# Value weights folded into the output weights in the opening of the attention: first loads right behind the keys', four staging tiles, stores on ScalarE's queue

## The chip, the cores and the metric

The kernel runs on one core of one Trainium2 chip. A core has five engines, each with its own queue of instructions: TensorE (PE, with its weight loads shown apart as PEld), VectorE (DVE), ScalarE (ACT), GpSimd (POOL) and SyncE (SP), which here only issues transfers. The metric is device time in microseconds (us) of one execution, as the median of several. A transfer issued from the queue of ScalarE or SyncE occupies that queue for the issue alone and lands later.

## The reference, cut to what matters

The reference is one encoder layer on 2048 tokens of width 1024. What the change touches is the latent attention (group B) and the output projection:

```python
q  = (rms_norm(c_q, g_cq) @ w_uq).reshape(B, S, 4, 192)
kv = (rms_norm(c_kv, g_ckv) @ w_ukv).reshape(B, S, 4, 256)   # c_kv: 128 wide
k_nope, v = kv[..., :128], kv[..., 128:]                      # per head: key part, value part
...
p = softmax(q @ k.T * scale)                                  # 4 heads, 2048 x 2048
y_b = p @ v                                                   # per head 2048 x 128
x = x + concat(y_a, y_b) @ w_out                              # w_out: 1024 x 1024
x = x + relu(rms_norm(x) @ w_ff1)**2 @ w_ff2
```

Here y_a is the output of the mLSTM (group A), four heads scanned in both directions over chunks of 128 tokens. The last 512 rows of w_out, 128 for each head, multiply y_b.

## The kernel before, in words

**Products.** All large products are in fp32r. A value is cut into a high part (a cast on ACT) and a low part (a subtraction on DVE or POOL, the helper `split`), and `mm3` (L68 to L71) makes one product of three matmuls: high by high, high by low, low by high.

**Phase A** takes 16 tiles of 128 tokens in two halves of eight: RMSNorm of x, h @ W_in in blocks of columns (the matmuls into tiles `pz`), a convolution for the mLSTM's queries and keys, and for each tile the work of the latent attention in four ticks. `mla_a1` (L309) normalises the two latents into `cn` (columns 256 to 383 are the latent of keys and values) and transposes them; `mla_a2` (L332) makes keys and values (two PSUM banks of 512 columns, weights `wukh`/`wukl` of 1024 columns) and queries (two banks of 384); `mla_b1` (L364) copies the values from PSUM to `vn` on ACT and stores them to `d_va`; `mla_b2` (L391) normalises, rotates and stores queries and keys. In phase A a scheduler orders the instructions by their dependences.

**The attention** (L975 on) is written in an order by hand. The steps g run from 0 to 255, two at a time. Sixteen steps make one block of 512 queries of one head, and four such blocks one head. A pair of steps issues, in this order: two score tiles (five matmuls each, L1090 to L1094, into one of three PSUM banks; DVE evicts each at L1095), two products of probabilities and values (`pv`, from g = 22 on), softmax exponentials on ACT (L1106), eight transposes of probabilities into two banks (L1137, then a cast `pth` on ACT and a subtraction `ptl` on DVE), and two steps of a second stream of work, the mLSTM, which starts with a prelude of 28 steps (`mlstm_prelude`, L603 to L722) that computes the gates. The prelude takes its PSUM tiles `pm` in turn from two banks (pool `c_psM`), so each new tile waits until the one before the last has been read. At the end of the prelude are the steps called p2, p1, p4 and p3 below: p2 is copied to `x2`, p1 to `x1`, p4 (L712, made from `x2`) to `rv`, and p3 (L717) is made from `x1`.

**Values and keys of a head.** `load_v` and `split_v` bring the values of one head in four tiles, 16 in all; each costs a cast on ACT and a subtraction on POOL. When a head ends, the keys of the next are split: those of step u = 4 and 5 of the pair on POOL, those of u = 6 on DVE. After the attention come the output projection (`OutProj`, with w_out's rows) and the feed-forward in Strassen form.

## Time and profile before

| what | value |
| --- | --- |
| median of three runs | 2545.64 us (2544.19, 2545.64, 2546.84) |
| the profiled execution, its own time | 2542.08 us |
| its span | 2540.3 us |
| granted TensorE clock | 1.00 throughout |
| busy: TensorE, weight loads | 99%, 83% |
| busy: VectorE, ScalarE, GpSimd | 68%, 51%, 15% |
| moved by DMA | 392.53 MB, 155 GB/s in the mean |

The span is what the profile covers; the execution's own time has 1.8 us more around it. A busy share counts the time in which at least one instruction of the engine was running. Matmuls are pipelined, so two matmuls of one stream overlap in the records: the spacing of their starts tells what one of them costs, and the duration in a group's row does not. Phase A covers the first 460 us, the attention with the mLSTM about 460 to 1110 us, output projection and feed-forward the rest.

### The profile page before, as it was taken

The numbers are of one execution on the slowest core, as the hardware profiler recorded it, in microseconds if no ns is written. First come the engines' busy times: TensorE is split into PE (matmuls) and PEld (weight loads), VectorE is DVE, ScalarE is ACT, GpSimd is POOL, SyncE is SP. The second block draws the span as 40 slices with busy tenths as digits, with TensorE's granted clock in tenths as the row PEclk, the third lists the DMA queues.
The fourth block names the chain that finished last, engine by engine and source line by source line (L and its number), as shares of the span: only waits on it lengthen the run. The fifth ranks groups of instructions, "written<-read, shape, count | busy, mean of one in ns | idle before, by whom it ended". The sixth has DMA issues, their size and how long they took to land. (4 is left out here: it accounts for less than half of the span.)

```text
span 2540.3 us, 35812 instructions
## 1 busy us (share of the span) xinstructions
PE 2523.7 (99%) x12380; PEld 2111.3 (83%) x12380; DVE 1726.1 (68%) x3286; ACT 1293.7 (51%) x2900; POOL 380.7 (15%) x428
## 2 busy tenths in 40 slices
PE   9999999999999999999999999999999999999999
PEld 7888888788888888888888888888888888888887
DVE  5585467766667667678788777977775577665433
ACT  6454444656767677674455555655554323332332
POOL 1211111223323332200000000000000232322000
PEclk9999999999999999999999999999999999999999
DMA  5434234355344343235786555654448544444552
GB/s 177 143 112 152 91 113 137 111 146 134 89 115 114 85 121 102 63 110 193 235 271 227 196 189 185 244 166 149 142 153 300 201 149 142 145 145 145 211 183 95
DMA packets 295931, 392.53 MB, mean 155 GB/s; under 512 B 32262, under 2 KB 176965, under 8 KB 295749
## 3 DMA queue, kind: packets, MB, share of 16 engines
q1 hardware_dynamic: 293284, 385.78, 48.0%
q10 hardware_dynamic: 2464, 4.46, 0.5%
q8 instruction: 97, 1.59, 0.3%
q14 instruction: 86, 0.70, 0.1%
HBM read 258.51 MB, written 131.64 MB: 154 GB/s over the span
## 5 line engine op out<-in xcount | busy, mean ns | idle before, releaser
L69 PE MATMUL pd<-w2h,uh 128*128 128x512 f32 x896 | 348.8, 389 | 0.1
L70 PE MATMUL pd<-w2l,uh 128*128 128x512 f32 x896 | 348.7, 389 | 0.0
L71 PE MATMUL pd<-w2h,ul 128*128 128x512 f32 x896 | 348.7, 389 | 0.0
L54 DVE TENSOR_TENSOR ul<-ur,uh 128x1024 fp32r<-128x1024 f32 x110 | 149.3, 1357 | 251.8 <-ACT uh L53 251.8
L53 ACT CAST uh<-ur 128x1024 fp32r<-128x1024 f32 x110 | 115.7, 1052 | 396.0 <-PE pd L70 382.4
L54 DVE TENSOR_TENSOR ptl<-ptp,pth 128x512 fp32r<-128x512 f32 x248 | 171.1, 691 | 190.0 <-ACT pth L53 188.9
L53 ACT CAST pth<-ptp 128x512 fp32r<-128x512 f32 x248 | 143.4, 578 | 157.7 <-PE ptp L1137 157.1
L2015 DVE TENSOR_TENSOR e<-pu,e 128x512 f32<-128x512 f32 x224 | 151.3, 689 | 88.7 <-PE pu L71 87.7
L69 PEld LDWEIGHTS pd<-w2h,uh 128*128 128x128 f32 x896 | 168.2, 188 | 35.4 <-DVE e L2015 0.5
L71 PEld LDWEIGHTS pd<-w2h,ul 128*128 128x128 f32 x896 | 168.2, 188 | 34.9
L70 PEld LDWEIGHTS pd<-w2l,uh 128*128 128x128 f32 x896 | 168.2, 188 | 34.8
L1106 ACT ACTIVATE p<-p,nm 128x512 f32<-128x512 f32 x256 | 185.8, 726 | 2.6 <-DVE nm L1099 2.6
L1095 DVE TENSOR_SCALAR_CACHE_REDUCE p<-ps 128x512 f32<-128x512 f32 x256 | 167.4, 682 | 15.2 <-PE ps L1094 15.1
L2179 POOL TENSOR_TENSOR r<-wr,r 128x512 f32<-128x512 f32 x48 | 81.5, 1697 | 621.1 <-DMA wr<-in_w 590.0
L69 PE MATMUL pz<-wh,hh 128*128 128x512 f32 (+1 forms) x384 | 149.5, 391 | 1.7 <-ACT vo L495 0.7
L71 PE MATMUL pz<-wh,hl 128*128 128x512 f32 (+1 forms) x384 | 150.0, 391 | 0.0
L70 PE MATMUL pz<-wl,hh 128*128 128x512 f32 (+1 forms) x384 | 149.2, 389 | 0.1
L2018 ACT ACTIVATE e<-e 128x512 f32<-128x512 f32 x128 | 80.9, 632 | 120.5 <-DVE e L2015 114.0
L1137 PE MATMUL ptp<-ident,p 128*128 128x128 f32 x992 | 130.6, 274 | 0.5 <-DVE ptl L54 0.3
L1137 PEld LDWEIGHTS ptp<-ident,p 128*128 128x128 f32 x992 | 113.6, 140 | 14.1 <-issue 1.4
L1090 PE MATMUL ps<-kh,qh 128*128 128x512 f32 x256 | 112.8, 441 | 2.4 <-DVE p L1095 2.4
L1883 ACT CAST r<-w1raw 128x512 fp32r<-128x512 f32 x104 | 64.6, 622 | 92.5 <-PE pu L71 92.5
(526 smaller groups left out, 6463.5 us busy)
## 6 DMA issues: line engine op xcount, KB each, us to landing
d_u<-e SPq DMA_DIRECT2D x224, 256.0 KB
ur<-d_u SPq DMA_DIRECT2D x110, 512.0 KB
wr<-in_w SPq DMA_DIRECT2D x96, 256.0 KB
w1raw<-in_w SPq DMA_DIRECT2D x42, 512.0 KB
raw<-in_w_in SPq DMA_DIRECT2D x48, 256.0 KB
r<-in_w SPq DMA_DIRECT2D x22, 512.0 KB
mb<-d_M SPq DMA_DIRECT2D x32, 256.0 KB
acc<-d_x SPq DMA_DIRECT2D x16, 512.0 KB
```

The lines of the kernel that those rows point to most:

```text
L53: r = nc.scalar.copy(hi, src)
L54: (eng or nc.vector).tensor_tensor(lo, src, hi.bitcast(F32), op=ALU.subtract)
L69: nc.tensor.matmul(out, ah, bh, start=first, stop=False, skip_group_check=more)
L70: nc.tensor.matmul(out, ah, bl, start=False, stop=False, skip_group_check=more)
L71: nc.tensor.matmul(out, al, bh, start=False, stop=last, skip_group_check=more)
L1090: nc.tensor.matmul(o, qh[:, qs], kh, start=True, stop=False)
L1095: nc.vector.tensor_scalar(p, o, SCALE, None, op0=ALU.mult, op1=ALU.max, accum_out=maxes[b, a][:, j:j + 1])
L1106: nc.scalar.activation(p, p, AF.Exp, bias=maxes[b, a], accum_out=dens[b][:, a, j:j + 1])
L1137: nc.tensor.transpose(pt[:, k, :], p[:, k * P:(k + 1) * P], c.ident)
L2015: nc.vector.tensor_tensor(out, o, t, op=ALU.add)
L2018: nc.scalar.activation(t, t, AF.Relu)
L2179: nc.gpsimd.tensor_tensor(R, wr, R, op=ALU.subtract)
```

## The change

The values of all heads are products of one latent with columns of w_ukv, so p @ v @ w_out can be taken as (p @ latent) @ (value columns of w_ukv @ w_out's rows). The change computes that second bracket once, 512 x 1024, in the opening of the attention, and stores it as `d_wv`.

- In phase A `mla_a2` makes the 512 key columns only, with one `mm3` in place of two. `vn` and `d_va` are gone; the latent goes from `cn` to `d_cn` by one transfer for each tile, issued on ACT's queue. `cn` has one buffer. The pool of x tiles has three buffers in place of two, and the tiles 8 to 15 are loaded earlier.
- In the attention the values are the latent itself, four tiles for all heads, loaded at g = 2 to 8 and split at g = 16 to 22. At a change of heads the keys of u = 4 are split on POOL and those of u = 5 and 6 on DVE.
- `value_loads` brings the value columns of w_ukv and two pieces of w_out behind the keys' loads. `value_rows` scales the columns by the gain on POOL, transposes and splits them, and then makes eight pieces, each with a split of a piece of w_out (ACT and POOL), one `mm3` into a `pm` bank, a copy by DVE into one of four staging tiles `wst`, and a store on ACT's queue. Its steps run with the prelude's; pieces 0 to 3 have their products at steps 8, 10, 12 and 14, pieces 4 to 7 at 22, 24, 26 and 28.
- Output projection and `load_b2` read `d_wv` where they read the last 512 rows of w_out. The reloads of the mLSTM's keys and values are issued one step earlier.

```diff
     c.d_kr = dr.tile([NH, ROPE, S], F32, name="d_kr")
-    c.d_va = dr.tile([S, 512], F32, name="d_va")
+    c.d_cn = dr.tile([S, P], F32, name="d_cn")
+    c.d_wv = dr.tile([NH * P, D], F32, name="d_wv")
     c.d_ya = dr.tile([S, 512], F32, name="d_ya")
...
         kp = pool("a_mla_const", 1, "right")
-        xp = pool("a_x", 2, "right")
+        xp = pool("a_x", 3, "right")
         zp = pool("a_zr", 8, "right")
...
                 raw = rp.tile([P, 512], F32, name="raw")
-                cs = slice(j * 512, (j + 1) * 512)
-                nc.sync.dma_start(raw, c.w_ukv[:, cs])
-                split(nc, wukh[:, cs], wukl[:, cs], raw, gcq[:, 2:3])
+                nc.sync.dma_start(raw, c.w_ukv[:, j * 512:(j + 1) * 512])
+                cs = slice(j * 256, (j + 1) * 256)
+                split(nc, *[w[:, cs].rearrange("p (h d) -> p h d", h=2) for w in (wukh, wukl)],
+                      raw.rearrange("p (h t d) -> p h t d", h=2, t=2)[:, :, 0, :], gcq[:, 2:3])
...
                 split(nc, ch, cl, pt[:, 0:3, :])
-            mla_env[t] = [zr, ms3, ch, cl]
+            mla_env[t] = [zr, ms3, ch, cl, cn]
...
-            zr, ms3, ch, cl = mla_env[t]
-            pk, pq = [], []
-            for j in range(2):
-                o = psM.tile([P, 512], F32, name="pm")
-                cs = slice(j * 512, (j + 1) * 512)
-                mm3(nc, o, ch[:, 2, :], cl[:, 2, :], wukh[:, cs], wukl[:, cs], True, True)
-                pk.append(o)
+            zr, ms3, ch, cl, cn = mla_env[t]
+            nc.scalar.dma_start(c.d_cn[t * P:(t + 1) * P, :], cn[:, 256:384])
+            pq = []
+            pk = psM.tile([P, 512], F32, name="pm")
+            mm3(nc, pk, ch[:, 2, :], cl[:, 2, :], wukh[:, 0:512], wukl[:, 0:512], True, True)
             for j in range(2):
...
             qs = [pq[h // 2][:, (h % 2) * DH:(h % 2 + 1) * DH] for h in range(NH)]
-            ks = [pk[h // 2][:, (h % 2) * 256:(h % 2) * 256 + NOPE] for h in range(NH)]
+            ks = [pk[:, h * NOPE:(h + 1) * NOPE] for h in range(NH)]
             for h in range(NH):
...
             rsqrt(c, r8, ms8, 8)
-            mla_env[t] = [zr, pk, qs, ks, r8]
+            mla_env[t] = [zr, qs, ks, r8]
...
-            tok = slice(t * P, (t + 1) * P)
-            zr, pk, qs, ks, r8 = mla_env[t]
-            vn = mp.tile([P, NH, DV], F32, name="vn")
-            for j in range(2):
-                nc.scalar.copy(vn[:, 2 * j:2 * j + 2, :],
-                               pk[j].rearrange("p (h d) -> p h d", h=2)[:, :, NOPE:])
-            nc.sync.dma_start(c.d_va[tok, :], vn.rearrange("p h d -> p (h d)"))
+            zr, qs, ks, r8 = mla_env[t]
             kpe = mp.tile([P, 1, ROPE], F32, name="kpe")
...
                 norm(t, xt)
+            elif 8 <= t < 13:
+                xts[t + 3] = load_x(t + 3)
...
                     tick(n + 6 * half)
+                    if half == 0 and blk == 2 and i == 3:
+                        for t in range(8, 11):
+                            xts[t] = load_x(t)
                     if half == 0 and blk == 2 and i >= 4:
...
         yield
+def value_place(n):
+    h, j = divmod(n, 2)
+    return slice(h * P, (h + 1) * P), slice(j * 512, (j + 1) * 512)
+def value_loads(c, stage):
+    raw = stage.tile([P, 512], F32, name="raw").rearrange("p (h d) -> p h d", h=NH)
+    c.nc.sync.dma_start(raw, c.w_ukv.rearrange("p (h t d) -> p h t d", h=NH, t=2)[:, :, 1, :])
+    pieces = [stage.tile([P, 512], F32, name="raw") for _ in range(2)]
+    for n, t in enumerate(pieces):
+        c.nc.sync.dma_start(t, c.w_out[512:][value_place(n)])
+    return raw, dict(enumerate(pieces))
+def value_rows(c, pool, psM, raw, pieces):
+    nc = c.nc
+    tile = pool.tile
+    outs = [tile([P, 512], F32, name=f"wst{i}") for i in range(4)]
+    wvh, wvl = (tile([P, NH, P], F32R, name=f"wv{u}") for u in "hl")
+    homes = [[tile([P, 512], F32R, name=f"wo{i}{u}") for u in "hl"] for i in range(2)]
+    raws = [tile([P, 512], F32, name=f"wraw{i}") for i in range(2)]
+    def part(n):
+        if n < 2 * NH:
+            split(nc, *homes[n % 2], pieces.pop(n), eng=nc.gpsimd)
+        if n + 2 < 2 * NH:
+            pieces[n + 2] = raws[n % 2]
+            nc.sync.dma_start(raws[n % 2], c.w_out[512:][value_place(n + 2)])
+    nc.gpsimd.tensor_scalar(raw, raw, c.vec[:, 10:11], None, op0=ALU.mult)
+    for _ in range(5):
+        yield
+    pt = psM.tile([P, 512], F32, name="pm").rearrange("p (k t) -> p k t", k=4)
+    for h in range(NH):
+        nc.tensor.transpose(pt[:, h, :], raw[:, h, :], c.ident)
+    yield
+    split(nc, wvh, wvl, pt)
+    part(0)
+    yield
+    yield
+    done = None
+    for n in range(2 * NH):
+        o = psM.tile([P, 512], F32, name="pm")
+        mm3(nc, o, wvh[:, n // 2, :], wvl[:, n // 2, :], *homes[n % 2], True, True)
+        yield
+        w = outs[n % 4]
+        nc.vector.tensor_copy(w, o)
+        part(n + 1)
+        yield
+        nc.scalar.dma_start(c.d_wv[value_place(n)], w)
+        for _ in range(6 if n == 3 else 0):
+            yield
...
         outs = [outer(kws.pop(ch), ld.pop(ch)[0]) for ch in grp]
+        for ch in grp:
+            if ch > 4:
+                ld[ch - 4] = mlstm_v(c, ch - 4), mlstm_k(c, ch - 4)
         yield
...
                 nc.sync.dma_start(c.d_C[ch - 1], new)
-                ld[ch - 4] = mlstm_v(c, ch - 4), mlstm_k(c, ch - 4)
             if k == 0 and n + 1 < len(groups):
...
-        def load_v(h, j):
-            raw = vraw[h, j] = rp.tile([P, 512], F32, name="raw").rearrange("p (k d) -> p k d", k=4)
-            nc.sync.dma_start(raw, c.d_va[j * 512:(j + 1) * 512, h * DV:(h + 1) * DV].rearrange(
-                "(k p) d -> p k d", p=P))
-
-        def split_v(h, j):
-            raw = vraw.pop((h, j))
+        def load_v(j):
+            raw = vraw[j] = rp.tile([P, 512], F32, name="raw").rearrange("p (k d) -> p k d", k=4)
+            nc.sync.dma_start(raw, c.d_cn[j * 512:(j + 1) * 512, :].rearrange("(k p) d -> p k d", p=P))
+        def split_v(j):
+            raw = vraw.pop(j)
             vh = vp.tile([P, 4, DV], F32R, name="vh")
...
             split(nc, vh, vl, raw, eng=nc.gpsimd)
-            V[h, j] = vh, vl
+            V[j] = vh, vl
...
         def pv(b, j, k):
-            h = b // NB
             if (j, k) == (0, 0):
...
             th, tl = pts[b, j]
-            vh, vl = V[h, j]
+            vh, vl = V[j]
             if b < N - 1:
...
                 nc.gpsimd.memset(t[:, :, DV:], 1.0)
-            ld = {ch: (mlstm_v(c, ch), mlstm_k(c, ch)) for ch in range(NT - 1, NT - 5, -1)}
-            yield from mlstm_prelude(c, psM)
+            with ExitStack() as s_fold:
+                fold = value_rows(c, pool("w_sb", 1, "left", s_fold.enter_context), psM, *early)
+                for n, _ in enumerate(mlstm_prelude(c, psM)):
+                    next(fold, None)
+                    if n == 10:
+                        ld = {ch: (mlstm_v(c, ch), mlstm_k(c, ch)) for ch in range(NT - 1, NT - 5, -1)}
+                    yield
+                for _ in fold:
+                    yield
             yield from mlstm_steps(c, pool("l_sb", 1, "left", sl.enter_context), psM, ld)
...
             split_k(0, j, nc.gpsimd if j == 2 else nc.vector)
-        load_v(0, 0)
-        load_v(0, 1)
+        early = value_loads(c, rp)
         work = mlstm()
-        def next_v(bp, j):
-            h = bp // NB + 1
-            if bp % NB == NB - 1 and h < NH:
-                split_v(h, j)
-                if j < 2:
-                    load_v(h, j + 2)
-
         for g0 in range(0, 16 * N, 2):
...
                     pv(bp, *divmod(n, 4))
-                    if n % 4 == 3:
-                        next_v(bp, n // 4)
             if g0 % 16 == 4 and g0 > 32:
...
                 if h < NH - 1 and i == 7 and u in (4, 5, 6):
-                    split_k(h + 1, u - 3, nc.vector if u == 6 else nc.gpsimd)
-                    if u == 6:
-                        load_v(h + 1, 0)
-                        load_v(h + 1, 1)
+                    split_k(h + 1, u - 3, nc.gpsimd if u == 4 else nc.vector)
                 if g >= 16:
...
                         load_k(h + 1, u - 3)
-                if g in (6, 8, 10, 12):
-                    split_v(0, g // 2 - 3)
-                    if g < 10:
-                        load_v(0, g // 2 - 1)
+                if g in (2, 4, 6, 8):
+                    load_v(g // 2 - 1)
+                if g in (16, 18, 20, 22):
+                    split_v(g // 2 - 8)
             if g0 == 16 * N - 10:
...
             raw = self.yp.tile([P, D], F32)
-            nc.sync.dma_start(raw, c.w_out[k * P:(k + 1) * P, :])
+            nc.sync.dma_start(raw, c.d_wv[(k - 4) * P:(k - 3) * P, :])
             raws += [raw[:, 0:512], raw[:, 512:]]
...
             self.c.nc.sync.dma_start(self.c.e[:, 4 * (1 - half) + k, :],
-                                     self.c.w_out[(4 + k) * P:(5 + k) * P, half * 512:(half + 1) * 512])
+                                     self.c.d_wv[k * P:(k + 1) * P, half * 512:(half + 1) * 512])
```

The following rows show three places of the program: the instructions of one engine in the order in which it takes them; a name in front of the arrow is the tile written (with its number), the names behind it are read.

First PE in phase A, for the key and value product of one tile of tokens (`cTh`, `cTl` are the transposed latent). Before:

```order
L69 MATMUL pm_921<-wukh_156,cTh_856 128x512
L70 MATMUL pm_921<-wukl_157,cTh_856 128x512
L71 MATMUL pm_921<-wukh_156,cTl_857 128x512
L69 MATMUL pm_925<-wukh_156,cTh_856 128x512
L70 MATMUL pm_925<-wukl_157,cTh_856 128x512
L71 MATMUL pm_925<-wukh_156,cTl_857 128x512
L69 MATMUL pm_929<-wuqh0_152,cTh_856 128x384
```

Now:

```order
L69 MATMUL pm_916<-wukh_157,cTh_854 128x512
L70 MATMUL pm_916<-wukl_158,cTh_854 128x512
L71 MATMUL pm_916<-wukh_157,cTl_855 128x512
L69 MATMUL pm_920<-wuqh0_153,cTh_854 128x384
L70 MATMUL pm_920<-wuql0_155,cTh_854 128x384
```

Three of the six matmuls are gone, and the queries' product follows.

Second PE in the opening of the attention, at the end of the prelude: p4 is the tile made from `rev` and `x2`, p3 the one from `x1` and `rev`, and `ptp` are transposes of probabilities. Before:

```order
L71 MATMUL pv_5466<-pth_5320,vl_5171 128x512
L712 MATMUL pm_5527<-rev_63,x2_5440 64x128 x2
L1137 MATMUL ptp_5533<-ident_58,p_5104 128x128 x4
L1137 MATMUL ptp_5541<-ident_58,p_5150 128x128 x4
L717 MATMUL pm_5549<-x1_5439,rev_63 128x192
L1090 MATMUL ps_5554<-kh_5032,qh_5237 128x512
```

Now:

```order
L71 MATMUL pv_5419<-pth_5261,vl_5271 128x512
L711 MATMUL pm_5492<-rev_63,x2_5393 64x128 x2
L69 MATMUL pm_5496<-wo1h_4985,wvh_4981 128x512
L70 MATMUL pm_5496<-wo1l_4986,wvh_4981 128x512
L71 MATMUL pm_5496<-wo1h_4985,wvl_4982 128x512
L1194 MATMUL ptp_5503<-ident_58,p_5003 128x128 x4
L1194 MATMUL ptp_5511<-ident_58,p_5058 128x128 x4
L716 MATMUL pm_5519<-x1_5392,rev_63 128x192
L1147 MATMUL ps_5527<-kh_4921,qh_5163 128x512
```

The product of a fold piece (`wo1h` by `wvh`) has come between p4 and the transposes. With two banks taken in turn, p3 now gets the bank of p4; before, it got that of p1, since p4 had the other.

Third DVE at the same place (`wst` is a staging tile of the fold). Before:

```order
L1095 TENSOR_SCALAR p_5504,mx_5505<-ps_5506 128x512
L1095 TENSOR_SCALAR p_5513,mx_5505<-ps_5514 128x512
L54 TENSOR_TENSOR ptl_5532<-ptp_5533,pth_5531 128x4x128
L54 TENSOR_TENSOR ptl_5532<-ptp_5541,pth_5531 128x4x128
L715 COPY rv_4972<-pm_5527 64x256
L1095 TENSOR_SCALAR p_5553,mx_5505<-ps_5554 128x512
```

Now:

```order
L1152 TENSOR_SCALAR p_5469,mx_5470<-ps_5471 128x512
L1152 TENSOR_SCALAR p_5478,mx_5470<-ps_5479 128x512
L54 TENSOR_TENSOR ptl_5502<-ptp_5503,pth_5501 128x4x128
L54 TENSOR_TENSOR ptl_5502<-ptp_5511,pth_5501 128x4x128
L714 COPY rv_4861<-pm_5492 64x256
L774 COPY wst1_4978<-pm_5496 128x512
L1152 TENSOR_SCALAR p_5526,mx_5470<-ps_5527 128x512
```

The copy `rv` that empties the bank of p4 stands where it stood, behind two subtractions `ptl`; the copy of the fold's piece has come behind it.

## Prediction

> **What bounds the kernel now.** I began with the page: its engines, then the chain that ended last.
>
> ```profile
> span 2540.3 us, 35812 instructions
> PE 2523.7 (99%) x12380; PEld 2111.3 (83%) x12380; DVE 1726.1 (68%) x3286; ACT 1293.7 (51%) x2900; POOL 380.7 (15%) x428
> ```
>
> PE is busy for 2523.7 of 2540.3 us, so all idle time of PE together is 16.6 us. Removing a wait can't bring more than that; removing matmuls can, as long as PE sets the pace where they stood. Next I asked for the windows by stage, to see where that holds, and for PE's waits.
>
> ```profile
> 0.00:460.00 460.00, 452.30 (x2248) 384.06 (x2248) 287.93 (x740) 225.19 (x652) 73.39 (x128) 1.00 0.42 134
> 530.00:1110.00 580.00, 579.16 (x3356) 492.94 (x3355) 393.54 (x1010) 397.88 (x1126) 161.69 (x171) 1.00 0.41 106
> 464.00:478.00 14.00, 13.31 (x59) 10.36 (x58) 12.90 (x39) 12.07 (x29) 6.35 (x5) 1.00 0.86 233
> PE pt L204 <- DMA rows<-in_g_mix: 4.5, 1, 4.5
> PE ps L1090 <- DVE p L1095: 2.4, 4, 1.3
> PE pt L325 <- DVE cn L321: 1.4, 1, 1.4
> ```
>
> The columns behind the length of a window are the busy time of PE, weight loads, DVE, ACT and POOL, then granted clock, DMA share and GB/s. In phase A (first row) PE lacks 7.7 us, of which 4.5 and 1.4 are two single waits, while DVE has 172 us free: PE sets the pace. The attention behind 530 lacks 0.84 us in 580. The opening of the attention, 464 to 478, is another matter: DVE is busy for 12.90 of 14 us and ACT for 12.07, and there scores wait for their evictions. The change takes matmuls out of the first place and puts work on all engines into the third.
>
> **Phase A: 48 matmuls fewer.**
>
> ```profile
> 308.72 0.39 PE L69 MATMUL pz<-wh,hh 128*128 128x512 f32 x1
> ...
> 309.86 0.39 PE L71 MATMUL pz<-wh,hl 128*128 128x512 f32 x1
> 310.08 0.49 PE L325 MATMUL pt<-ident,cn 128*128 128x128 f32 x3
> ...
> L69 PE MATMUL pm<-wukh,cTh 128*128 128x512 f32 x32 | 13.0, 408 | 0.0
> L369 ACT COPY vn<-pm x32: 351/365/401, 62.7 to 420.6; 128x256 f32<-128x256 f32 x32
> ```
>
> Durations of matmuls overlap, so I price by spacing: from 308.72 to 310.08 stand six matmuls of 128x512, 0.227 us apart. The group of L69 has 32 for 16 tiles, two for each; the same holds for L70 and L71. Half of the 96 go: 48 x 0.227 = **-10.9 us**. The 32 copies of `vn` (0.365 us each) leave ACT, which had 235 us free in phase A, so they bring nothing; 16 transfers issued on ACT's queue come in their place, and those cost nothing either while ACT has that room (below 0.33 us each, as the issue of `d_sg` at 459.73 shows in the timeline quoted further down). The earlier loads of x would save a wait for x, and PE's list has none of any size: 0. Should `cn`, which has one buffer, wait for its transfer, DVE would stand for about 2 us; a tile comes every (420.6 - 62.7)/15 = 23.9 us, and I keep 0.
>
> **The fold: 24 matmuls and 4 transposes more.** Eight pieces of three matmuls, 24 x 0.227 = 5.4; four transposes of 128x128 at 0.11 us (493.01, 493.12, 493.23 below) 0.44. Together **+5.9 us**. Its stores are covered by the queues, and its readers (the output projection, behind 1110 us) come hundreds of us later.
>
> **The bank of p4.** In the order, p3 now takes the bank that p4 had, and waits until the copy `rv` has read it. How late is that? These are PE, ACT and DVE at the place:
>
> ```profile
> 493.01 0.27 PE L702 MATMUL pm<-ident,u 128*128 128x128 f32 x1
> 493.12 0.27 PE L702 MATMUL pm<-ident,w 128*128 128x128 f32 x1
> 493.23 0.27 PE L702 MATMUL pm<-ident,gd 128*128 128x128 f32 x1
> 493.34 0.49 PE L1137 MATMUL ptp<-ident,p 128*128 128x128 f32 x3
> ...
> 497.97 0.65 PE L712 MATMUL pm<-rev,x 128*64 128x128 f32 x4
> 498.55 1.09 PE L1137 MATMUL ptp<-ident,p 128*128 128x128 f32 x8
> 499.48 0.49 PE L717 MATMUL pm<-x,rev 128*128 128x192 f32 x2
> 499.67 0.53 PE L1090 MATMUL ps<-kh,qh 128*128 128x512 f32 x1
> ...
> 499.29 0.58 ACT L53 CAST pth<-ptp 128x512 fp32r<-128x512 f32 x1 [1.79 <-PE ptp L1137]
> 499.78 0.72 ACT L1106 ACTIVATE p<-p,nm 128x512 f32<-128x512 f32 x1
> ...
> 493.14 0.42 DVE L699 COPY x<-pm 128x256 f32<-128x256 f32 x1
> ...
> 501.10 0.69 DVE L54 TENSOR_TENSOR ptl<-ptp,pth 128x512 fp32r<-128x512 f32 x1 [0.50 <-ACT pth L53]
> 501.71 0.41 DVE L715 COPY rv<-pm 64x256 f32<-64x256 f32 x1
> ```
>
> `rv` stands on DVE behind two subtractions, the second of which waits for a cast that stands on ACT behind an exponential. So it ends at 501.71 + 0.41 = 502.12, and p3 was issued at 499.48, 2.64 us earlier. The product of piece 5 ahead of the transposes moves both ends by the same 0.68 us. Behind p3 on PE stand the next scores, which have no use for `rv`, yet wait with it. The same kind of wait, smaller, stands at piece 4, whose bank is free when `x2` is copied, 493.14 + 0.42 = 493.56, where PE arrives at 493.34: 0.2. Together **+2.8 us**. It lies between 0.2 (if ACT's and DVE's queues have run ahead) and 3.5 (if the copy of piece 4 and its split come between); I take the row.
>
> **The opening, steps 6 to 17.** Before, PE stalls here twice, since scores wait for DVE:
>
> ```profile
> 470.17 0.39 PE L1094 MATMUL ps<-rl,qr 128*128 128x512 f32 x1
> 471.25 0.50 PE L1090 MATMUL ps<-kh,qh 128*128 128x512 f32 x1 [0.69 <-DVE p L1095]
> ...
> 478.56 0.40 PE L1094 MATMUL ps<-rl,qr 128*128 128x512 f32 x1
> 480.30 0.50 PE L1090 MATMUL ps<-kh,qh 128*128 128x512 f32 x1 [1.34 <-DVE p L1095]
> ...
> 476.20 3.45 DVE L671 TENSOR_TENSOR_SCAN mr<-g 1x15 f32<-1x15 f32 x8
> 459.73 0.33 ACTq L497 DMA_DIRECT2D d_sg<-vo  x1
> 467.69 0.60 ACT L53 CAST vh<-raw 128x512 fp32r<-128x512 f32 x1
> 468.20 0.72 ACT L1106 ACTIVATE p<-p,nm 128x512 f32<-128x512 f32 x1
> L54 POOL TENSOR_TENSOR vl<-raw,vh 128x512 fp32r<-128x512 f32 x16 | 20.6, 1285 | 80.2 <-ACT vh L53 58.8 <-PE ps L1094 13.2 <-DMA mb<-d_M 7.9
> ```
>
> In spacing the two stalls cost (471.25 - 470.17 - 0.23) + (480.30 - 478.56 - 0.23) = 2.4 us. Pieces 0 to 3 come into this stretch. They put 4 x 0.68 + 0.44 = 3.2 us on PE (counted above) and five operations of 0.69 us (one split, four copies, priced by the subtractions of that size) or 3.5 us on DVE, which had 1.1 us left in 14: DVE's lead does not grow smaller. A piece's operand takes a cast (0.60) and a POOL subtraction (1.29), 1.9 us, and its cast stands behind two exponentials (1.8 us with their reads) in a pair of steps that lasts about 3.1 us: PE waits up to 0.6 us for each of the four, 2.4 in all. I take these in place of the old stalls, since PE can't wait for both at once, and add the 0.3 by which DVE gets more than PE: **+0.3 us**, between -2.4 (the pieces fill the old stalls) and +2.4 (both stand).
>
> **The boundary and the values' casts.** The order has the last `pz` matmuls ahead of the first scores now, where 48 of them stood behind the first scores before; so the first evictions have no PE work over them, and the last transposes of phase A come behind two scores. A score's eviction has the size of a subtraction `ptl`, 0.69 us, two of them 1.4: +0.5, between 0 and 1.5. The four casts of the values (0.60 each) move from g = 6 to 12 to g = 16 to 22, among the casts `pth` that transposes wait for: +0.3, between 0 and 1.4. Together **+0.8 us**.
>
> **The changes of heads.**
>
> ```profile
> 765.88 1.27 POOL L54 TENSOR_TENSOR kl<-raw,kh 128x512 fp32r<-128x512 f32 x1 [9.04 <-ACT kh L53]
> ...
> 769.66 2.53 DVE L890 TENSOR_TENSOR rd<-rd,gn 128x4 f32<-128x4 f32 x2
> ...
> 769.62 1.30 POOL L54 TENSOR_TENSOR rl<-raw,rh 128x512 fp32r<-128x512 f32 x1
> ...
> 773.14 0.47 PE L1090 MATMUL ps<-kh,qh 128*128 128x512 f32 x1 [0.23 <-DVE p L1095]
> ...
> 777.93 0.66 PE L1137 MATMUL ptp<-ident,p 128*128 128x128 f32 x4 [0.33 <-DVE ptl L54]
> ```
>
> Two tiny DVE operations took 2.53 us while POOL ran key subtractions, and the score's eviction came late: PE stood idle for 0.23 and 0.33 us. PE's list of waits has no other of such a size at a change of heads. Now POOL splits one set of keys where it split two, and 12 of the 16 value subtractions are gone, so I let these 0.56 us go: **-0.6 us**.
>
> **Sum:** -10.9 + 5.9 + 2.8 + 0.3 + 0.8 - 0.6 = -1.7 us. The profiled execution took 2542.08 us (its span and 1.8 around it), 3.6 under the median of three, so it would go to 2540.4 and the median to 2545.64 - 1.7 = **2543.9 us**. A measurement of this kernel can tell about 0.2%, 5.1 us, from no change; this is within it.
>
> **Rivals.**
>
> - *The waits are covered.* The p3 wait shrinks to 0.2 since DVE and ACT run ahead, the pieces fill the old stalls. For it: ACT stood idle for 1.79 us ahead of `pth` at 499.29. Against it: it was idle because the transposes it waits for had just come, so it can't run ahead of them. With the boundary free as well, -10.9 + 5.9 + 0.2 - 2.4 - 0.6 = -7.8: 2537.8 us. With only one of the two, about 2540.
> - *DVE and POOL block each other (slower).* The place is the change of heads, three times. In the rows above an operation of 128x4 on DVE took 1.27 us, the length of a POOL subtraction beside it. If each of the four key subtractions that are now DVE's waits out one POOL operation, 4 x 1.3 = 5.2 us a change, less the 1.5 us or so that three score banks give PE, 3 x 3.7 = 11 us come on: -1.7 + 0.6 + 11 = +9.9, 2555.5 us. It decides from where POOL still works when DVE's first subtraction comes; before, POOL's key subtractions ran from 765.88 on, four of some 1.3 us, and two of these now leave it. [...]
> - *The matmuls taken out of phase A come back as waits there.* If DVE or ACT set the pace of phase A, -10.9 would shrink, to about half if the boundary at 460 us is set by the last stores; -1.7 + 5.4 = +3.7, 2549.3 us. Against it speaks PE's 452.30 of 460.
> - *The change doesn't do what it says*: the pieces' operands are not there by the steps meant, and PE waits a full 1.9 us for each of eight, 15 in place of 2.4; about 2557 us. The loads stand right behind the keys' and the steps give them some 10 us, so I hold this small.
>
> **How the numbers follow.** My forecast has 0.50, the covered waits 0.28 (half of that under 2540.5), the loss in phase A 0.08, the lock 0.09, late pieces 0.05. The bounds of the unknown terms, all low or all high, give 2545.64 - 7.8 = 2537.8 and 2545.64 - 10.9 + 5.9 + 3.5 + 2.4 + 2.9 = 2549.4. The range 2537.8 to 2549.4 leaves out the lock and the late pieces. Faster by over 0.2% (below 2540.5): part of the covered waits and the low end of the forecast, 0.25. Slower by over 0.2% (above 2550.7): 0.12. Within: 0.63.
>
> **What would show it.** In the changed profile: 48 records of the key product at L69 to L71 less the missing ones, and the first score about 11 us earlier; p3 (now L716) with an idle time of 2 to 3 us ahead of it, put down to DVE `rv`; waits of `pm` matmuls for POOL `wo` of 0.2 to 1 us in the opening; and no more than 1 us of PE idle at each change of heads. No wait at p3 means the first rival; DVE subtractions `kl` of over 1.2 us at the changes mean the second. What would make the prediction wrong beyond its range is a place that I didn't price: a reordering of phase A, or a transfer that comes late for the four latent tiles at g = 16.

## The result and the profile after

The changed kernel takes 2549.51 us in the median of 22 runs (2547.62 to 2552.48), the kernel before 2544.42 us in the same 22 rounds: a ratio of 1.0019, with a 95% interval of 1.0013 to 1.0026. It is slower by 5.1 us, where 1.7 us less were forecast, and lies just above the range. The two profiled executions are 6.8 us apart in span (2540.3 and 2547.1 us): that of before was a quick one, 2542.08 us against its median of 2544.42. Positions below come from these two; the sizes that decide come from medians.

The head of the page of the changed kernel:

```profile
span 2547.1 us, 35692 instructions
PE 2523.9 (99%) x12360; PEld 2109.0 (83%) x12360; DVE 1741.0 (68%) x3301; ACT 1286.9 (51%) x2865; POOL 369.0 (14%) x419
```

And PE's list of waits (what was waited for, us in total, times, longest):

```profile
PE pt L205 <- DMA rows<-in_g_mix: 4.5, 1, 4.5
PE pm L716 <- DVE rv L714: 2.6, 1, 2.6
PE pm L70 <- POOL wo0l L54: 1.7, 2, 0.9
PE ptp L1194 <- DVE ptl L54: 1.4, 2, 0.8
PE pm L70 <- POOL wo1l L54: 0.9, 2, 0.7
```

PE is busy as long as before and the span is longer: matmuls went, waits came. The wait at p3 (L716 now) is the 2.6 us that the row of before had given. Where the time went is told by the starts of the same score tile in both traces (the n-th matmul of L1090, L1147 now, counted from 0):

| score tile | before, us | after, us | after less before |
| --- | --- | --- | --- |
| 2 (behind phase A) | 460.03 | 451.53 | -8.5 |
| 8 | 467.00 | 458.97 | -8.0 |
| 16 | 477.31 | 476.18 | -1.1 |
| 24 | 494.13 | 493.83 | -0.3 |
| 28 | 504.28 | 509.84 | +5.6 |
| 64 | 599.38 | 605.81 | +6.4 |
| 128 | 771.51 | 778.60 | +7.1 |
| 140 | 805.56 | 810.99 | +5.4 |
| 255 | 1110.33 | 1115.81 | +5.5 |

Phase A gave 8.5 us, and 40 us later all was gone and 6 more. One trace is good to about 1 us in such a place: the four kernels with the same phase A (the changed one and, below, e1, e4 and g2) start score tile 8 between 458.6 and 460.4 us. Between the tiles 8 and 16 of the changed kernel stand the pieces 0 to 3 of the fold, twelve matmuls or 2.7 us, and PE's waits for their operands, 3.1 us:

```profile
461.69 0.51 PE L69 MATMUL pm<-wo0h,wvh 128*128 128x512 f32 x1 [0.28 <-ACT wo0h L53]
463.05 0.50 PE L70 MATMUL pm<-wo0l,wvh 128*128 128x512 f32 x1 [0.86 <-POOL wo0l L54]
466.53 0.50 PE L70 MATMUL pm<-wo1l,wvh 128*128 128x512 f32 x1 [0.21 <-POOL wo1l L54]
470.28 0.50 PE L69 MATMUL pm<-wo0h,wvh 128*128 128x512 f32 x1 [0.17 <-ACT wo0h L53]
471.62 0.50 PE L70 MATMUL pm<-wo0l,wvh 128*128 128x512 f32 x1 [0.84 <-POOL wo0l L54]
475.61 0.50 PE L70 MATMUL pm<-wo1l,wvh 128*128 128x512 f32 x1 [0.72 <-POOL wo1l L54]
```

The last 1.3 us of the pair's 6.8 come in the feed-forward, which is the same in both; I take them for the difference of the two executions. The windows show a thing that the prediction does not have (columns as before: PE, weight loads, DVE, ACT and POOL busy, clock, DMA share, GB/s):

```profile
480.00:500.00 20.00, 18.63 (x99) 14.63 (x97) 13.77 (x35) 14.31 (x35) 8.52 (x7) 1.00 0.43 91
500.00:520.00 20.00, 17.38 (x85) 14.42 (x86) 10.87 (x26) 9.07 (x22) 4.16 (x5) 0.91 0.24 64
```

PE's timeline in the second of them (start, duration, engine, line):

```profile
502.70 0.98 PE L716 MATMUL pm<-x,rev 128*128 128x192 f32 x2 [2.62 <-DVE rv L714]
503.23 0.88 PE L1147 MATMUL ps<-kh,qh 128*128 128x512 f32 x1
503.90 0.63 PE L1148 MATMUL ps<-kl,qh 128*128 128x512 f32 x1
504.33 0.63 PE L1149 MATMUL ps<-kh,ql 128*128 128x512 f32 x1
...
505.61 0.60 PE L1147 MATMUL ps<-kh,qh 128*128 128x512 f32 x1
506.04 0.41 PE L1148 MATMUL ps<-kl,qh 128*128 128x512 f32 x1
506.29 0.39 PE L1149 MATMUL ps<-kh,ql 128*128 128x512 f32 x1
```

The granted clock is 0.91 in the mean of these 20 us. The matmuls stand 0.43 us apart until 506.04 and 0.23 us behind it. The clock stood at half from 502.64 to 506.05 us, 3.4 us, so that some 1.7 us were lost on top of the 2.6.

### The profile page after: what moved, and what is told of

It is laid out like the page before. It is cut to its first block, busy times and chain, and to the rows that moved or that the text cites. A ratio compares the mean times of both kernels' runs of the same rounds, so it can differ in the third digit from the quotient of the medians.

```text
span 2547.1 us, 35692 instructions
## 1 busy us (share of the span) xinstructions
PE 2523.9 (99%) x12360; PEld 2109.0 (83%) x12360; DVE 1741.0 (68%) x3301; ACT 1286.9 (51%) x2865; POOL 369.0 (14%) x419
## 5 line engine op out<-in xcount | busy, mean ns | idle before, releaser
L1147 PE MATMUL ps<-kh,qh 128*128 128x512 f32 x256 | 113.1, 442 | 0.0
```

Of the source, the lines that this page charges most:

```text
L1147: nc.tensor.matmul(o, qh[:, qs], kh, start=True, stop=False)
```

## The experiments

All times are medians beside the kernel before (2544.3 to 2545.0 us in these rounds); the interval of each ratio reaches 0.0008 to 0.0013 to either side.

### First four: the opening taken apart

Piece 5 later (e1), the same bank wait in the kernel before (e2), no fold (e3), the operands earlier (e4):

```diff
-        for _ in range(6 if n == 3 else 0):
+        for _ in range({3: 6, 4: 2}.get(n, 0)):            # e1
...
         nc.vector.tensor_copy(rv, p4)
+        nc.tensor.transpose(bank()[:, 0:P], u, c.ident)    # e2, on before
...
-                    next(fold, None)                       # e3; w_out read in place of d_wv
...
-    homes = [[tile([P, 512], F32R, name=f"wo{i}{u}") for u in "hl"] for i in range(2)]
+    homes = [[tile([P, 512], F32R, name=f"wo{i}{u}") for u in "hl"] for i in range(4)]   # e4
...
-        part(n + 1)
+        part(n + 2)
```

> The changed kernel with the product of piece 5 (and the pieces behind it) two steps later, so that p3 takes the bank of piece 4 and not that of p4. Theory (the miss sits in the opening; p3's wait for rv of 2.6 us costs a further 1.7 us, since the granted clock falls to half behind it): the wait and the stretch at half clock both go, 4.3 us faster than the changed kernel, about 2545.2 us, and PEclk in 500-520 is 1.00. Rival (the clock falls because the whole opening feeds PE too thinly, not for this one wait): the wait goes, 2.6 us, but a stretch at half clock stays somewhere between 460 and 520, about 2546.9 us. Rival (the wait moves to the next reader of that bank): no change, 2549.5 us.

> The kernel before with one more bank taken between p4 and p3 (a transpose of 128x128 that nobody reads), so that p3 must wait for rv as in the changed kernel, and nothing else is changed. Theory: PE stands idle for 2.6 us at p3 and the granted clock falls to half for about 3 us behind it, 0.1 for the transpose, 2.6 + 1.7 + 0.1 = 4.4 us slower than before, about 2548.8 us. Rival (the clock belongs to the thin opening of the changed kernel): the wait alone, 2.7 us, about 2547.1 us at a clock of 1.00.

> The changed kernel without the fold: the eight pieces, their splits, copies and stores are left out, and the output projection reads the rows of w_out instead of their products (that part of the computation is left out). Theory (phase A gives its 10.9 us, the fold in the opening costs them again): -10.9 for the matmuls, -0.6 at the changes of heads, +2 at the boundary, so 9.5 us faster than before, about 2535 us; so the fold costs 14.5 us, where its matmuls take 5.9. Rival (phase A or the rest of the attention gives part of the gain back, and the fold costs little more than its matmuls): about 2549.5 - 5.9 - 4.3 = 2539.3 us or more.

> The changed kernel with four pairs of tiles for the split pieces of w_out in place of two, and each piece split one piece earlier (three steps ahead of its product in place of one). Theory (PE waits for the operands of pieces 0 to 3, 4.4 us by the spacing of its matmuls): most of these waits go, 3 us faster than the changed kernel, about 2546.5 us, if DVE doesn't then stop the scores; p3's wait stays. Rival (DVE is the bound of the opening, so PE waits for an eviction in place of the operand): the operands' waits go and waits of the scores for DVE p come, under 1 us in all, about 2549 us.

| run | us | ratio, interval |
| --- | --- | --- |
| e1 | 2550.09 | 1.0020, 1.0011 to 1.0029 |
| e2 | 2544.75 | 0.9998, 0.9989 to 1.0007 |
| e3 | 2539.66 | 0.9979, 0.9970 to 0.9988 |
| e4 | 2550.16 | 1.0022, 1.0013 to 1.0031 |

All four theories missed; in e3 and e4 the rival was the nearer (2539.3 and 2549 us). **e1** did what it was to do: no wait at p3, and score 32 starts at 514.72 us, where the changed kernel has 520.83. Then it lost 3.7 of these 6.1 us again between the score tiles 60 and 64, and the rest by the last one. The place, in SP's and PE's timelines:

```profile
580.33 8.02 SPq L1094 DMA_DIRECT2D raw<-d_kr x2
588.44 0.56 SPq L784 DMA_DIRECT2D v<-d_v  x1
...
595.38 0.96 PE L928 MATMUL pm<-v,mb 128*128 128x129 f32 x4 [2.70 <-DMA v<-d_v]
```

With the mLSTM two steps later, a load of v stood on SP's queue behind a key load that was held for 8 us. **e2** had no wait at p3 at all: presumably the bank that nobody read came free at once and p3 took that one. It tells nothing on the clock. **e4** lost its operand waits to waits for DVE: the scores waited 2.8 us in all for evictions (longest 1.9), as the rival had it.

**e3** is the one that changes the question. Without any fold the kernel keeps only 4.9 us of the 10.9. These are PE, ACT and DVE of e3, where it lost them:

```profile
458.23 0.39 PE L1151 MATMUL ps<-rl,qr 128*128 128x512 f32 x1
461.31 0.79 PE L1147 MATMUL ps<-kh,qh 128*128 128x512 f32 x1 [2.69 <-DVE p L1152]
461.91 0.63 PE L1148 MATMUL ps<-kl,qh 128*128 128x512 f32 x1
...
454.24 0.59 ACT L460 COPY kt<-pt 128x512 f32<-128x512 f32 x1 [3.08 <-DMA d_k<-kt]
458.31 0.26 ACT L472 COPY kt<-pt 2x128 f32<-2x128 f32 x1 [3.48 <-DMA d_k<-kt]
458.47 0.30 ACT L634 ACTIVATE e<-f 128x128 f32<-128x128 f32 x1
458.79 1.28 ACT L635 ACT_TABLE_LOAD   x1
460.08 0.31 ACT L635 ACTIVATE e<-e 128x128 f32<-128x128 f32 x1
...
460.43 0.23 DVE L637 TENSOR_SCALAR w<-e 128x128 f32<-128x128 f32 x1 [4.28 <-ACT e L635]
460.57 0.68 DVE L1152 TENSOR_SCALAR_CACHE_REDUCE p<-ps 128x512 f32<-128x512 f32 x1
```

And the window behind the wait:

```profile
461.00:468.00 7.00, 6.69 (x17) 5.25 (x18) 5.46 (x19) 6.96 (x16) 0.00 (x0) 0.53 0.81 240
```

Read the timeline from PE to its cause. The score at 461.31 waited for an eviction on DVE; that stood behind `w`, which waited for the exponential `e` on ACT; that stood behind a table load and the copy into `kt`, the tile by which the last convolved channel goes to memory. `kt` has one buffer, so each copy waits until the store of the last has landed, 3.1 and 3.5 us. The chain is on ACT and DMA, and taking matmuls off PE does not shorten it: in before the last such copy started at 460.18, here at 458.31, while PE came 7.4 us earlier. Behind the wait stand 6.8 us at half clock, 460.69 to 467.51 us (0.53 in the mean of 7).

### Second four: the clock, and the chain at the end of phase A

```diff
-  kt = ep.tile([P, 4, P], F32, name="kt", bufs=1)
+  kt = ep.tile([P, 4, P], F32, name="kt", bufs=2)          # g1 on e3, g5 on before
...
-        for _ in range(6 if n == 3 else 0):
+        for _ in range(6 if n == 5 else 0):                # g2
...
+        spare = bank()[:, 0:P]                             # g4, on before, behind p4;
+        nc.tensor.transpose(spare, u, c.ident)             # read only behind rv
```

> The kernel without the fold (e3: eight pieces, splits, copies and stores left out, output projection on w_out itself), and the tile kt of the convolution's transposes with two buffers in place of one. Theory (the end of phase A is a chain on ACT: each copy into kt waits 3 to 3.5 us for the store of the last, the prelude's exponential and table loads stand behind, DVE's next evictions behind those; PE waits 2.7 us and then runs at half clock for 6 us, 3 us more): the waits of kt go, the first exponential comes 3 to 6 us earlier, PE's wait goes with its half clock, 5 us faster than e3's 2539.7, about 2534.5 us. Rival (the chain is held by the table loads and the DVE work at the end of phase A, not by kt): 0 to 1 us.

> The changed kernel with pieces 4 and 5 at steps 16 and 18, ahead of the prelude's p2, and the pause behind piece 5; pieces 6 and 7 stay at 26 and 28, so the mLSTM keeps its steps. Theory (p3's wait with its half clock cost 4 to 6 us; e1 gained these up to step 48 and lost them at 592, where a load of v stood on SP's queue behind a key load that waited 8 us for a staging tile): no wait at p3, no wait for v, 4.5 us faster than the changed kernel, about 2545 us. Rival (whatever is gained in the opening is lost again at the next place where transfers are late): 2549.5 us, with a wait of PE for v or a stretch of half clock behind 520.

> The kernel before with one more bank between p4 and p3, written by a transpose and read by a DVE copy only behind rv, so that p3 has to take p4's bank and to wait for rv. Theory (a wait of over 2.5 us halves the clock for some 3 us by itself): PE idle for 2 to 2.7 us at p3, then matmuls of 128x512 0.43 us apart for 3 us; 2.6 + 1.6 + 0.1 = 4.3 us slower than before, 2548.8 us. Rival (the half clock of the changed kernel has another cause): 2.7 us slower, 2547.2 us, at a clock of 1.00.

> The kernel before with two buffers for kt, a control for g1. Theory (before, PE still has phase A's matmuls while ACT waits for kt, so it costs little): 0 to 1 us faster than before, 2543.5 to 2544.5 us. Rival (a second buffer helps either kernel alike): 3 us or more faster.

| run | us | ratio, interval |
| --- | --- | --- |
| g1 | 2530.89 | 0.9946, 0.9934 to 0.9959 |
| g2 | 2548.41 | 1.0013, 1.0004 to 1.0021 |
| g4 | 2548.61 | 1.0016, 1.0007 to 1.0025 |
| g5 | 2542.60 | 0.9992, 0.9983 to 1.0001 |

**g4** gives the price of the bank wait: one wait added to the kernel before costs 4.1 us by the medians (1.8 to 6.4 by the interval), where 4.3 or 4.4 were expected; between the score tiles 24 and 28 of the traces it is 4.5. The time alone would not exclude the rival's 2.7, but the rival has a clock of 1.00, and the trace has half clock, here from 504.80 to 508.21 us. PE's timeline of g4:

```profile
504.44 0.64 PE L719 MATMUL pm<-x,rev 128*128 128x192 f32 x2 [2.62 <-DVE rv L717]
504.70 0.80 PE L1093 MATMUL ps<-kh,qh 128*128 128x512 f32 x1
505.30 0.63 PE L1094 MATMUL ps<-kl,qh 128*128 128x512 f32 x1
505.73 0.63 PE L1095 MATMUL ps<-kh,ql 128*128 128x512 f32 x1
...
508.26 0.40 PE L1096 MATMUL ps<-rh,qr 128*128 128x512 f32 x1
```

**g1** gave 8.8 us on e3, more than the 5 expected: with two buffers the scheduler also puts 48 `pz` matmuls behind the first four score matmuls again, as in before. Score 8 starts 10.0 us earlier than before and the gain stays. So g1 changes two things at once, the waits for kt and the order at the end of phase A. ACT at its end:

```profile
448.15 0.58 ACT L460 COPY kt<-pt 128x512 f32<-128x512 f32 x1 [4.49 <-DMA d_k<-kt]
448.63 0.25 ACT L472 COPY kt<-pt 2x128 f32<-2x128 f32 x1
450.94 0.31 ACT L634 ACTIVATE e<-f 128x128 f32<-128x128 f32 x1 [1.57 <-DVE f L631]
```

One wait put down to kt's store is still there, but it ends 6.1 us earlier than in e3, the second copy follows at once, and the first exponential comes at 450.94 in place of 458.47 us and waits for its own operand alone. **g5**: the second buffer brings the kernel before 1.9 us by the medians, between 4.3 us and nothing by the interval, so it is not worth g1's 8.8 there. **g2** won 1.1 us, not clear of the noise, where 4.5 were expected: p3 no longer waits, but pieces 4 and 5 met the prelude's DVE work, and the operands of the pieces cost more (POOL `wo0l` 2.6 us, three times, where the changed kernel has 1.7 and two).

### Third four: the chain mended in the changed kernel

The edits are those above put together: h1 is the changed kernel with two buffers for kt, g3 that with g2's order, h3 with e1's, h4 with e4's.

> The changed kernel with two buffers for kt. With it the scheduler of phase A also puts the last 48 pz matmuls behind the first four score matmuls again, as before. Theory (the 10.9 us of phase A were lost at its end, where ACT waits for kt's stores, and the opening's pieces then waited behind ACT; g1 kept 12 us without the fold where e3 kept 3.5): the first scores come 10 us earlier than before and stay so until the fold; the fold then costs 10 us, p3's wait with its half clock among them: 2530.9 + 10 = 2541 us, 8.5 us faster than the changed kernel. Rival (the fold's operands, not kt, hold the opening: ACT and POOL can't split the pieces in time however early phase A ends): 2 to 3 us faster than the changed kernel, about 2547 us.

> As h1 (two buffers for kt), with pieces 4 and 5 ahead of p2 as in g2, so that p3 doesn't wait for rv. Theory: 4 us less than h1 for p3's wait and its half clock, some 2 us of it given back by pieces 4 and 5, which meet the prelude's DVE work as they did in g2: about 2539 us. Rival (as in g2, all is given back): 2541 us, as h1.

> As h1, with piece 5 two steps later as in e1, so that p3 doesn't wait for rv and the mLSTM comes two steps later. Theory: 4.3 us less than h1 in the opening, and the wait for v behind a key load on SP's queue at about 580 us comes as in e1, 2.7 us and some 3 us of half clock: about 2541 us, as h1, with no wait at p3. Rival (that wait was an accident of e1): 2537 us.

> As h1, with four pairs of tiles for the pieces of w_out and each split one piece earlier, as in e4. Theory (with ACT free in time, what is left of the pieces' waits is the split right ahead of its product): 2 us less than h1, 2539 us. Rival (as in e4, DVE stops the scores instead): as h1, 2541 us.

They took 2544.36 us (h1, ratio 0.9999), 2542.81 (g3, 0.9992, 0.9984 to 1.0001), 2546.27 (h3) and 2545.52 (h4). h1 is 5.2 us faster than the changed kernel: the end of phase A, with its chain and its order, was the larger part of the loss. In the traces h1 is 1.4 us ahead of it at score tile 8 and 3.1 at tile 16: ACT comes to the pieces 3.2 us earlier, and PE hardly waits for the operands of pieces 0 and 1. ACT's cast for piece 0 in the changed kernel and in h1:

```profile
461.01 0.62 ACT L53 CAST wo0h<-raw 128x512 fp32r<-128x512 f32 x1
...
457.84 0.62 ACT L53 CAST wo0h<-raw 128x512 fp32r<-128x512 f32 x1
```

But h1 stays 13.5 us above g1, where the fold's matmuls take 5.9; my 10 was short, and with it the forecasts of the other three. In h3 the wait for v came again (2.8 us), as expected. g3 gains 1.6 on h1, which the intervals do not tell from nothing, and h4 gains nothing.

### Last five: why the fold costs more than its matmuls

```diff
-                    k2 = ep.tile([P, 4, P], F32, name="kt", bufs=1)[0:2, 0, :]
+                    k2 = ep.tile([P, P], F32, name="k2")[0:2, :]            # k_e3_k2
...
-        if n < 2 * NH:
+        if n < 2:                                                           # j3, on g3
             split(nc, *homes[n % 2], pieces.pop(n), eng=nc.gpsimd)
...
+                    if half == 1 and blk < 2 and i % 2 == 1:                # m1; j1, j2 alike
+                        fold(blk * 4 + i // 2)
```

In j1, j2 and m1 `fold` makes one piece in phase A: load, split (ACT, POOL), `mm3` into the bank that `mla_a2` no longer uses, DVE copy, store on ACT's queue.

> The kernel without the fold (as e3: the eight pieces are left out, the output projection reads w_out itself), with a tile of its own for the last two columns of each transposed channel in place of kt's one buffer. The order of the matmuls at the end of phase A stays that of e3. Theory (ACT's waits of 3.1 and 3.5 us for d_k's stores hold the prelude's exponential, and with it DVE and the scores): these waits go, PE's 2.7 us and the 3 us of half clock behind it go, 5 us faster than e3, about 2534.7 us. Rival (the scheduler's order holds it, and two buffers helped through the order alone): as e3, 2539.7 us.

> Two buffers for kt, and the fold made in phase A: the value columns are transposed where the weights are split, and one piece is made at every second tile of the first two blocks of the second half, into the fourth bank of the pool that the keys and queries use. Nothing of the fold is left in the attention. Theory (the fold costs its matmuls where PE is the bound and the others are free): 2530.9 + 5.9 = 2536.8 us, 7.7 us faster than before. Rival (its splits, copies and stores cost PE time wherever they stand): 2530.9 + 10 or more, 2541 us or more.

> As j1, with one buffer for kt as in the changed kernel. Theory (the end of phase A holds ACT whatever the place of the fold): e3 and the fold's matmuls, 2539.7 + 5.9 = 2545.6 us. Rival (with PE longer busy in phase A its end comes out as before, since ACT's chain has 6 us more time): 2537 to 2540 us.

> As g3 (two buffers for kt, pieces 4 and 5 ahead of p2), with the splits of pieces 2 to 7 left out: the products are made from the first two pieces again (that part of the computation is left out). Theory (PE waits for the operands of the pieces, 5 us by the spacing of its matmuls in g3): 4 to 5 us faster than g3, about 2538 us. Rival (DVE, with its copies and evictions, is what holds the opening; PE then waits for it): as g3, 2542.8 us.

> As j1 (two buffers for kt, the fold in phase A), with the value columns loaded again and transposed at the start of the second half, and the eight pieces at every second tile of its first two blocks. Theory (the fold costs its matmuls where PE is the bound): the first half as in g1, 2530.9 + 5.9 = 2536.8 us, faster than before and than the changed kernel. Rival (the fold displaces other work in phase A wherever it stands, through the schedule): 2541 us or more, with waits of PE in phase A of 4 us or more beyond g1's.

| run | us | ratio, interval |
| --- | --- | --- |
| k_e3_k2 | 2536.46 | 0.9971, 0.9960 to 0.9982 |
| j1 | 2545.12 | 1.0004, 0.9995 to 1.0012 |
| j2 | 2546.76 | 1.0009, 1.0001 to 1.0018 |
| j3 | 2538.74 | 0.9978, 0.9969 to 0.9987 |
| m1 | 2540.87 | 0.9987, 0.9978 to 0.9996 |

**k_e3_k2** keeps e3's order of matmuls at the end of phase A and takes two of ACT's waits away: 3.2 us of e3's loss go by the medians, where 5 were expected; the intervals of the two runs overlap, and the traces are 4.4 us apart at the last score. Its timeline shows what remains. The next table load on ACT follows 3.57 us behind the exponential, and `w` on DVE, with the evictions behind it, waits for 3.32 us; the trace puts both down to d_k's store from `kt` (why they need that store is not shown):

```profile
454.24 0.31 ACT L635 ACTIVATE e<-e 128x128 f32<-128x128 f32 x1
458.12 1.28 ACT L640 ACT_TABLE_LOAD   x1 [3.57 <-DMA d_k<-kt]
...
458.16 0.23 DVE L637 TENSOR_SCALAR w<-e 128x128 f32<-128x128 f32 x1 [3.32 <-DMA d_k<-kt]
458.30 0.68 DVE L1152 TENSOR_SCALAR_CACHE_REDUCE p<-ps 128x512 f32<-128x512 f32 x1
...
459.05 0.50 PE L1147 MATMUL ps<-kh,qh 128*128 128x512 f32 x1 [1.74 <-DVE p L1152]
459.39 0.39 PE L1148 MATMUL ps<-kl,qh 128*128 128x512 f32 x1
```

PE's wait is 1.74 in place of 2.69 us, and no half clock follows. So the two waits taken away hold about a third of the 8.8 us between e3 and g1, and by the traces kt's store holds more than that: of the 3.4 us that k_e3_k2 lies behind g1 at score tile 8, 1.3 stand at tile 2 and 2.0 come behind it, where PE waits for the eviction behind `w`. What the order of the end of phase A costs by itself stays open, since no run has e3's order without any wait for kt.

**j3** leaves six of eight operand splits out and gains 4.1 us on g3: 4 to 5 were expected, so the splits, with the waits for them, are about that share of the fold's cost. **j1** does not tell what it was to tell: at 232 us PE waited for ACT's `hh`, 2.7 us, with half clock behind it (0.93 in the mean from 235 to 260 us), presumably because the fold's transposes in the first half made the x tiles of the second late. **j2** has the same trouble there (waits of 2.7 and 1.7 us, 6.8 us at half clock), so its 2546.8 us, near the 2545.6 of its theory, is luck. The end of its phase A speaks for its rival: with one buffer it is 0.6 us behind j1 at score tile 2 and 0.6 at the last score, PE has no wait above 0.4 us from 450 to 470 us, and the `pz` matmuls stand behind the first scores as in before. So one buffer costs where PE's work has been taken out of phase A, and not where the fold has been put in. **m1** has the transposes in the second half and no such wait in the first. It is faster than before by 3.4 us (0.13%) and 8.6 us faster than the changed kernel, and the only complete kernel here whose interval lies below 1. Against g1 the fold costs 10.0 us there, not 5.9, so the rival (2541) was the nearer: four more us of waits stand between 399 and 418 us (operands and `cn`), part of them half clock (0.64 in the mean from 414 to 418 us).

## Why the prediction was wrong, step by step

**Phase A, -10.9: right as work, wrong as gain.** In g1, where the order of the end is that of before, score tile 1 starts at 447.77 us, where before has 458.19: 10.4 us earlier, though its first `pz` matmul came 0.4 us later (7.42 and 6.99 us). The sign that the prediction gave for it, the first score 11 us earlier, did not come: in the changed kernel score tile 0 starts 2.0 us later than before (447.02 and 445.01 us), with the last `pz` matmuls now ahead of it. The one buffer of `cn`, for which the prediction weighed 2 us and kept 0, held nothing up on DVE: its 16 transfers were issued in 0.33 us each (median) and landed 1.5 us from the issue, and DVE's only idle time ahead of L323 is 0.3 us, put down to POOL.

**The boundary, +0.8: the step that failed.** It priced two evictions and four casts, with an upper bound of 2.9. e3 shows what it had to price: without 10.9 us of matmuls phase A no longer ends on PE, but on a chain over ACT, DVE and the stores of kt. The terms without the fold were -10.9 + 0.8 - 0.6 = -10.7; e3 measured -4.9. That is 5.8 of the 6.8 us by which the sum was off, and the second buffer, with the order that comes with it, returns 5.2 of them in the changed kernel (h1). In the changed kernel itself the loss does not stand in one wait as in e3: 2.4 us of the 10.9 are missing at score tile 2 already, and most of the rest comes as late operands of the first pieces (3.1 us, above). How much of it is the order and how much the waits for kt is not shown. The prediction named a reordering of phase A as a thing that it had not priced. I had asked whether PE sets the pace of phase A and read it from 452.30 busy of 460 us, a mean over the stage; its last 15 us have another limit. I had also written down that removed copies bring ACT nothing, since it had 235 us free. It has time in these 15 us too, but spends it on waits for the stores of kt (3.1 and 3.5 us in e3), with the rest of its queue behind. The third rival, phase A's gain coming back as waits, had 8% of the chance and named the last stores at the boundary, which is near to what e3 shows. That its 2549.3 us fits so well is luck: it has no half clock at p3 and no late operands beyond the forecast's.

**The fold's matmuls, +5.9, and the bank of p4, +2.8.** The wait at p3 was forecast at 2.64 us and is 2.62. What followed it was not: half clock for 3.4 us, 1.7 us more. g4 measured 4.1 for the whole.

**The opening, +0.3: too small, and hidden in the sum.** After less e3, the fold costs 9.9 us, and 5.9 + 2.8 + 0.3 = 9.0 were forecast; this nearness is partly luck, since in the changed kernel the fold fills the hole that the chain leaves (its trace has no wait like the 2.69 us of e3). With the chain mended (h1 less g1) it costs 13.5: its matmuls 5.9, p3 with the clock 4.1, and 3.5 left, near the 4.1 of the operands that j3 measured in g3. I had set the operands' waits of 2.4 against the old stalls of 2.4; g1 shows that the old stalls vanish without the fold as well.

**The changes of heads, -0.6: not seen.** PE's idle time at the change at tile 128 was 0.56 us before (0.23 and 0.33) and is 0.56 us now. In the profiled pair the changed kernel is 5.6 us behind at tile 127 and 5.4 at tile 140; the 7.1 at tile 128 lie between. No run took this edit alone. The blocking of DVE by POOL, the rival with 9%, showed its sign but not its price, and that POOL was the cause is not shown. Two of the twelve key subtractions that DVE has at the changes took 1.88 and 1.78 us where the shortest take 0.68, the first of them while POOL made `iz` (773.05 to 775.62 us):

```profile
774.29 1.88 DVE L54 TENSOR_TENSOR kl<-raw,kh 128x512 fp32r<-128x512 f32 x1 [0.53 <-ACT kh L53]
...
777.43 0.66 PE L1194 MATMUL ptp<-ident,p 128*128 128x128 f32 x4 [0.56 <-DVE ptl L54]
```

PE stood for 0.56 us behind it, where the rival had 3.7 for each change.

## What to carry to other kernels

A stage in which one engine is busy for 98% (452.30 of 460 us of phase A) can still end on another one, as in e3 on ACT and the stores of kt: before pricing work removed from it, follow the last 20 us of the stage on every engine, single-buffered stores above all. The wait of 2.6 us here lost 1.7 us more by half clock in the changed kernel (3.4 us of it) and none in h4, so price such a wait with a range. And the operands prepared one step ahead of their products were late here, where their engines stood behind other work: the splits cost 4.1 us (j3), of the 5.0 us of matmuls that the change saves net. Preparing them one piece earlier did not help (e4, h4), since DVE then held the scores (2.8 and 2.5 us of waits for evictions).

## What of the hardware was not expected

The clock behind a wait was not a matter of the wait's length alone here. In the profiled executions p3's wait of 2.62 us was followed by half clock in the changed kernel, in h1 and in g4, and not in h4 and e4. In e4 the clock fell at 478.21 us instead, behind a wait of 1.85 us for an eviction that ended at 477.01. PE of h4, with the same wait at p3:

```profile
500.20 0.56 PE L716 MATMUL pm<-x,rev 128*128 128x192 f32 x2 [2.62 <-DVE rv L714]
500.47 0.53 PE L1148 MATMUL ps<-kh,qh 128*128 128x512 f32 x1
500.83 0.39 PE L1149 MATMUL ps<-kl,qh 128*128 128x512 f32 x1
501.06 0.40 PE L1150 MATMUL ps<-kh,ql 128*128 128x512 f32 x1
```

Here the matmuls stand 0.23 us apart at once. A wait of 1.74 us (k_e3_k2, above) was followed by full clock as well. It differs between executions of one kernel, too: this one of h4 is the only one of its eleven with a mean granted clock of 1.000, the others have 0.998 or 0.999. In h1 the two executions at 1.000 took 2542.5 us in the mean and the nine at 0.999 took 2545.0; only the profiled one shows where the clock fell. Where a trace has it fall between the start and the end, it stayed at half for 3.41 us, or for 6.82 and 6.83 us (e3, j2). The matmuls of 128x512 behind these waits have two spacings, 0.43 and 0.23 us. Why the same 2.62 us was followed by half clock in three of these traces and not in two is not shown, and no limit in length is either: 1.85 us had half clock behind it (e4), 2.62 us had none (h4). The 2.5 us in g4's theory was my estimate, from the 2.62 us of the changed kernel and the 2.69 us of e3.
